# Stick-breaking mask by a restarting scan, value projections with 512 columns, and queued work shared out anew, in a two-layer hybrid decoder trunk

## The chip, the cores and the metric

The kernel runs on one core of a Trainium2 chip (trn2). The metric is the device time of one execution in microseconds. TensorE (PE in the profile) multiplies matrices and writes PSUM banks, VectorE (DVE) and ScalarE (ACT) read PSUM and SBUF, GpSimd (POOL) works on SBUF, SyncE (SP) issues the transfers from HBM.

## The reference

Two layers, each three sub-layers on a sequence of 512 tokens with 1024 features, all float32: a half-step SwiGLU, a token mixing, a half-step SwiGLU, each between two RMS norms. The mixing adds three attentions, each with a sigmoid gate: stick-breaking (8 heads of 64), forgetting (8 heads of 64) and attention to a memory of 256 tokens (4 heads of 128). Stick-breaking is the one whose mask changes:

```python
z = jnp.einsum('bhqd,bhkd->bhqk', qb, k).astype(jnp.float32) * scale
mask = key_pos[None, :] < q_pos[:, None]
log_beta = jax.nn.log_sigmoid(z)
log_not = jnp.where(mask, log_beta - z, 0.0)
log_between = lax.cumsum(log_not, axis=3, reverse=True) - log_not
w = jnp.where(mask, jnp.exp(log_beta + log_between), 0.0)
```

So a query sees the keys before it, and the weight of a key is its own sigmoid times the product of (1 - sigmoid) over the keys between. With s = softplus(z) this is exp(z - (sum of s from the key up to the last visible one)).

## The kernel before

**Numbers.** Every float32 operand of a product is split into a high and a low part in the PE's f32r format (`split`, L179: a cast on ScalarE, a difference on VectorE), and a product is three matmuls, high x high, high x low, low x high (`mm3`, L206). A weight *unit* (`Unit`, L235) is 1024 elements a partition (512 KB): it is fetched into one of two `raw` buffers by SyncE and split into one of four `wh` and four `wl` buffers. SBUF tiles of one tag share a ring of buffers (`BUFS`, L102), PSUM has two rings of four banks: `mm` for projections and outputs, `z` for scores and transposes.

**The queue.** TensorE's order is written out by a planner. `Queue` (L363) holds jobs, each a list of weight units and a generator; each step of the generator emits some matmuls and yields the time it thinks they take (columns / 2370, in us; "planned us" below). When a job begins, its units are loaded and up to four units of the next jobs are loaded ahead. Beside the queue run *chains* (L446, `weave`): a chain emits its own work on TensorE, yields `("pe", us)`, and then `("wait", us)`: for so long the planner fills in steps of the queue, up to a `limit` (an index into the queue). When the queue has come to the limit, the plan skips the rest of the wait and the chain's next piece follows at once. The waits are constants: `W_H`, `W_U` (L602) at the seams between sub-layers, `W_MM0`, `W_MM1`, `W_SB0`, `W_SB1`, `W_FL`, `W_FX0`, `W_FX1`, `W_K` (L1076 to L1080) in the mixing. `Q.past(n, us)` runs the queue to job n and `us` into it; `Q.until(n)` to job n. Instructions of the other engines are put in order by the framework's scheduler.

**The seams.** When a half of the down projection of a token tile is done (`down`, L777), a chain (L591) computes its residual and norm, waits `W_H` and `W_U[t]`, transposes the tile on TensorE (`turned`, L586) and splits the result. The next SwiGLU begins with a pair of column blocks in two halves of the tokens (`halved`, L631), the second of which needs all four tiles.

**The mixing** (`mixing`, L1108) queues per layer: memory keys and values (`mem_kv`, L872), memory queries, q, k and v of the stick-breaking and the forgetting heads, gates and branch products (`merge`), then the output projection. Heads go in pairs p = 0 to 3 with j = 0, 1. Over the queue run the chains: four memory heads (`mem_head`), eight stick heads (`stick_head`, L950), eight forgetting heads (`fox_head`, L999). Each has three pieces on TensorE: scores (`zm`, `zs`, `zf`), transposes of the weights (`ptm`, `pts`, `ptf`; `transposed`, L940), product with the values (`pvm`, `pvs`, `pvf`; `attend`, L926). The first stick head's scores are begun during the last memory head's wait (L1301).

**Values.** `vproj` (L897) puts two token tiles of 256 value columns side by side into one PSUM bank; for every tile and feature block the activations are the stationary operand and 256 weight columns stream past (L907 to L909). Memory values go through it in two groups of columns (`values`, L884). Stick and forgetting values too, in groups of two head pairs (`v_half`, from L1145, called by `project_v`, L1173): stick group 0 before head 0, stick group 1 behind head 0's other work, forgetting group (1,0) later. The first forgetting group goes with the eight forget-gate columns (`v_gates`, 264 columns).

**The mask.** `masks16` holds two bf16 triangles of 0 and -1e30 (`more_constants`, L138). A stick head writes them into three PSUM banks by four matmuls with the identity (L958), then adds the scores (L964). Per bank, ScalarE and VectorE form softplus (L969 to L972), `tensor_tensor_scan` (L976) runs from the last key backwards with state = 1 x state + s, and L978 and L979 subtract and take Exp. A masked score of -1e30 has a softplus of 0 and an Exp of 0. Forgetting heads use the other triangle in the same way (L1005).

Of the kernel before, what the change touches and what calls it, by code (L numbers as in the profile page):

```python
# [22 lines left out]
def kernel(  # L23
# [66 lines left out]
    ident16 = cst.tile([P, P], BF16, name="ident16")  # L90
# [4 lines left out]
    masks16 = cst.tile([P, P + 1], BF16, name="masks16")  # L95
    causal16, strict16 = masks16[:, 0:P], masks16[:, 1:P + 1]
# [41 lines left out]
    def more_constants():  # L138
        later = tc.keep_in_program_order
        later(nc.vector.tensor_copy(ident16[:], ident[:]))  # L140

        t0 = tmp("c0")
        later(nc.vector.memset(t0[:, :P + 1], 0.0))
        nc.gpsimd.affine_select(out=t0[:, 256:257 + P], in_=t0[:, :P + 1], pattern=[[-1, P + 1]], compare_op=ALU.is_ge,
                                fill=-1e30, base=0, channel_multiplier=1)
        later(nc.vector.tensor_copy(masks16[:], t0[:, 256:257 + P]))
# [455 lines left out]
    W_H, W_U = 4.8, (8.0, 7.0, 6.5, 6.5)  # L602
# [269 lines left out]
    def mem_kv(l, mn, ks, vs):  # L872

        mact = lambda k: (mn[0][:, k], mn[1][:, k])

        def keys(c, un):
            kt = stile([P, 2, 2, M], "v", f"mk{l}_{c}")
            for m in range(2):
                pt = pbank("mm", f"pmk{l}_{c}_{m}")
                yield from gemm(pt[:, :M], un, m, mact)  # L880
                split(kt[:, 0, m], kt[:, 1, m], pt[:, :M])
            ks.append(kt)

        def values(c, un):  # L884
            vt = stile([P, 2, MT, 256], "v", f"mv{l}_{c}")
            pt = yield from vproj(un, mact, range(MT), f"pmv{l}_{c}")
            split(vt[:, 0].rearrange("p t c -> p (t c)"), vt[:, 1].rearrange("p t c -> p (t c)"), pt[:])
            vs.append(vt)
# [4 lines left out]
        un = [wpair(w_mem_kv[l], ND, 512 + c * 256, f"mv{l}_{c}") for c in range(2)]  # L893
        Q.add(un[0], lambda: values(0, un[0]))
        return lambda: Q.add(un[1], lambda: values(1, un[1]))

    def vproj(units, act, tiles, name):  # L897

        pt = pbank("mm", name)
        for i, t in enumerate(tiles):  # L900
            o = pt[:, i * 256:(i + 1) * 256]
            ts_ = slice(t * P, (t + 1) * P)
            for un in units:
                for k in range(un.nk):
                    ah, al = act(un.k0 + k)
                    first = i == 0 and un.k0 + k == 0
                    nc.tensor.matmul(o, ah[:, ts_], un.h[:, k], start=first, stop=False)  # L907
                    nc.tensor.matmul(o, ah[:, ts_], un.l[:, k], start=False, stop=False)
                    nc.tensor.matmul(o, al[:, ts_], un.h[:, k], start=False, stop=(i == 1 and un.k0 + k == ND - 1))  # L909
                    yield 768 * PE_US  # L910
        return pt
# [14 lines left out]
    def attend(pv, j, vts, pj, tri, ot, name):  # L926

        r, rl, _ = HEAD_ROWS[j]
        for kt in range(NT):
            lo = QLO[kt]  # L930
            v = vts[kt // 2][:, 2 * (kt % 2) + pj, 2 * j:2 * j + 2, :].rearrange("p e c -> p (e c)")
            for part in range(2):
                nc.tensor.matmul(pv[:, lo:], v, tri_part(tri, part, kt, kt * P - lo), start=(kt == 0 and part == 0),
                                 stop=(kt == NT - 1 and part == 1), skip_group_check=True)
# [15 lines left out]
    def stick_head(q, k, vts, pj, j, ot, name, late):  # L950
# [5 lines left out]
        for rows, pz in zip(banks, pzs):  # L956
            for n, (i, at) in enumerate(rows):
                nc.tensor.matmul(pz[:, at + i * P:at + (i + 1) * P], ident16[:], strict16, start=n == 0, stop=False,  # L958
                                 skip_group_check=True)
        for rows, pz in zip(banks, pzs):  # L960
            for i, at in rows:
                wp = max((i + 1) * P, 256)
                for kk in (j, 2 + j):
                    nc.tensor.matmul(pz[:, at:at + wp], q[:, j, i * P:(i + 1) * P], k[:, kk, :wp], start=False,  # L964
                                     stop=(kk == 2 + j), skip_group_check=True)
# [19 lines left out]
        attend(pbank("mm", "pv" + name), j, vts, pj, wt, ot, name)  # L985
# [13 lines left out]
    def fox_head(q, k, vts, pj, j, qk, ot, name, ahead):  # L999

        rc = slice(0, 104 if j == 0 else P)
        ptile = {}
        pzs = [pbank("z", f"z{name}_{i}") for i in range(NT)]
        for i, pz in enumerate(pzs):
            nc.tensor.matmul(pz[:, i * P:(i + 1) * P], ident16[:], causal16, start=True, stop=False,  # L1005
                             skip_group_check=True)
        for i in reversed(range(NT)):
# [6 lines left out]
            st = sb.tile([P, 2], F32, tag="st", bufs=8, name=f"st{name}_{i}")  # L1014
# [12 lines left out]
        attend(pbank("mm", "pv" + name), j, vts, pj, tri, ot, name)  # L1027
        yield ("pe", 1.2)

    def mem_head(q, ks, vs, hd, ot, name, begun):  # L1030
# [37 lines left out]
        for kt in range(MT):  # L1068
            c = slice(kt * S, (kt + 1) * S)
            vc = slice((hd % 2) * P, (hd % 2 + 1) * P)  # L1070
            v = vs[hd // 2]
            mm3(pv[:], v[:, 0, kt, vc], v[:, 1, kt, vc], tri[:, 0, c], tri[:, 1, c], kt == 0, kt == MT - 1)
# [3 lines left out]
    W_SB0, W_SB1 = 11.0, 4.7  # L1076
    W_FL = 3.0
    W_FX0, W_FX1 = 6.0, 4.2
    W_MM0, W_MM1 = 6.0, 6.0
# [28 lines left out]
    def mixing(l, src, ks, vs, rest, dst):  # L1108
# [36 lines left out]
        def v_half(br, c, un):  # L1145
            for i in range(NT // 2):
# [3 lines left out]
                pt = yield from vproj(un, act, (2 * i, 2 * i + 1), f"pv{l}_{br}_{c}_{i}")  # L1150
# [88 lines left out]
        marks["values"] = rest()  # L1239
# [8 lines left out]
        marks[heads[0]] = len(Q.jobs)  # L1248
        for i, (br, _) in enumerate(heads):
# [6 lines left out]
            if i % 2 == 0 and i + 2 < len(heads):  # L1256
# [17 lines left out]
        def run():  # L1274
# [5 lines left out]
            def mems():  # L1280
# [13 lines left out]
                for i in range(NMH):  # L1294
# [24 lines left out]
            def fox(at, j):  # L1319
                pre(at, j)  # L1320
                p = FOX[at]
                return fox_head(st["q", 1, p], st["k", 1, p], st["v", 1, p // 2], p % 2, j, fx[p, j], st["o", 1][p],
# [117 lines left out]
    for l in LAYERS:  # L1440
# [3 lines left out]
        rest = mem_kv(l, mn, *kvs[l])  # L1444
        mb = mixing(l, subs[i + 1], *kvs[l], rest, subs[i + 2])
# [38 lines left out]
```

## Time and profile before

| | |
|---|---|
| median of 3 runs | 2443.98 us (2442.83 to 2444.6) |
| the profiled execution | 2443.11 us |
| its span, first to last instruction | 2441.3 us |
| granted TensorE clock, mean | 0.999 |
| instructions | 30918, of them 12167 matmuls |
| from HBM | 272.20 MB, 114 GB/s over the span, reads and writes |

In the rows of a timeline stand the start from the span's start, the duration in us, engine, line, operation, what it writes <- reads, the shape, how many rows were merged, and in brackets the idle time before it with what ended it. Matmuls overlap in the pipeline: a printed duration is longer than the distance to the next one. In a row of groups stand, after the count, busy us, mean ns of one, and idle us of the engine before them. In a row of waits stand who waited for whom, total us, how often, and the longest. Tile names are without buffer numbers (`pv` is a bank of a value projection, `pmv` of a memory value projection).

### The profile page before, as it was taken

The numbers are of one execution on the slowest core, as the hardware profiler recorded it, in microseconds if no ns is written. First come the engines' busy times: TensorE is split into PE (matmuls) and PEld (weight loads), VectorE is DVE, ScalarE is ACT, GpSimd is POOL, SyncE is SP. The second block draws the span as 40 slices with busy tenths as digits, with TensorE's granted clock in tenths as the row PEclk, the third lists the DMA queues.
The fourth block names the chain that finished last, engine by engine and source line by source line (L and its number), as shares of the span: only waits on it lengthen the run. The fifth ranks groups of instructions, "written<-read, shape, count | busy, mean of one in ns | idle before, by whom it ended". The sixth has DMA issues, their size and how long they took to land.

```text
span 2441.3 us, 30918 instructions
## 1 busy us (share of the span) xinstructions
PE 2429.5 (100%) x12167; PEld 2062.0 (84%) x12167; DVE 1544.3 (63%) x2182; ACT 1173.4 (48%) x1897; POOL 72.6 (3%) x129
## 2 busy tenths in 40 slices
PE   9999999999999999999999999999999999999998
PEld 8888889888888888888888888899888888888887
DVE  4364777677876653646644546866778866445466
ACT  4333365567655543333433333546676655333333
POOL 0000000001110000000000000000001100000000
PEclk9999999999999999999999999999999999999999
DMA  4333445222213433333424343442232243333433
GB/s 139 116 126 130 136 158 155 74 74 70 87 61 120 139 104 112 124 127 127 158 87 130 113 144 131 166 128 70 70 96 69 71 137 129 96 130 105 145 115 128
DMA packets 238597, 280.50 MB, mean 115 GB/s; under 512 B 8666, under 2 KB 188914, under 8 KB 238452
## 3 DMA queue, kind: packets, MB, share of 16 engines
q1 hardware_dynamic: 238356, 278.50, 35.5%
q8 instruction: 95, 1.56, 0.3%
q14 instruction: 50, 0.41, 0.0%
q0 software_dynamic: 96, 0.03, 0.0%
HBM read 272.20 MB, written 6.29 MB: 114 GB/s over the span
## 4 chain that ended last, share of the span: by engine, by line
PE 94%; DVE 2%; ACT 2%; DMA 1%; issue 1%; DVEq 0%; ACTq 0%
PE pg L208 4%; PE pg L210 4%; PE pg L209 4%; PE pgc L208 3%; PE pgc L210 3%; PE pgc L209 3%; PE puc L208 3%; PE puc L209 3%; PE puc L210 3%; PE pga L208 3%; PE pga L210 3%; PE pua L210 3%; PE pga L209 3%; PE pda L209 3%; PE pua L209 3%; PE pda L208 3%
## 5 line engine op out<-in xcount | busy, mean ns | idle before, releaser
L208 PE MATMUL pg<-us_a,wh_wg 128*128 128x512 f32 x384 | 150.7, 392 | 0.0
L209 PE MATMUL pg<-us_a,wh_wg 128*128 128x512 f32 x384 | 149.8, 390 | 0.0
L210 PE MATMUL pg<-us_a,wl_wg 128*128 128x512 f32 x384 | 149.6, 390 | 0.0
L208 PE MATMUL pgc<-us_b,wh_gc 128*128 128x512 f32 x320 | 124.5, 389 | 0.0
L209 PE MATMUL pgc<-us_b,wh_gc 128*128 128x512 f32 x320 | 124.5, 389 | 0.0
L210 PE MATMUL pgc<-us_b,wl_gc 128*128 128x512 f32 x320 | 124.5, 389 | 0.0
L210 PE MATMUL puc<-us_b,wl_uc 128*128 128x512 f32 x320 | 124.5, 389 | 0.0
L208 PE MATMUL puc<-us_b,wh_uc 128*128 128x512 f32 x320 | 124.5, 389 | 0.0
L209 PE MATMUL puc<-us_b,wh_uc 128*128 128x512 f32 x320 | 124.5, 389 | 0.0
L183 DVE TENSOR_TENSOR wl_uc<-raw_uc,wh_uc 128x1024 fp32r<-128x1024 f32 x44 | 53.9, 1225 | 107.3 <-ACT wh_uc L182 107.3
L183 DVE TENSOR_TENSOR wl_ua<-raw_ua,wh_ua 128x1024 fp32r<-128x1024 f32 x44 | 53.8, 1224 | 99.1 <-ACT wh_ua L182 99.1
L182 ACT CAST wh_uc<-raw_uc 128x1024 fp32r<-128x1024 f32 x44 | 46.3, 1052 | 88.8 <-PE pgc L209 37.7
L183 DVE TENSOR_TENSOR wl_gc<-raw_gc,wh_gc 128x1024 fp32r<-128x1024 f32 x40 | 48.8, 1223 | 62.1 <-ACT wh_gc L182 61.8
L210 PE MATMUL pda<-wh_da,ala 128*128 128x512 f32 x224 | 87.1, 389 | 0.0
L209 PE MATMUL pda<-wl_da,aha 128*128 128x512 f32 x224 | 87.1, 389 | 0.0
L208 PE MATMUL pdc<-wh_dc,ahc 128*128 128x512 f32 x224 | 87.1, 389 | 0.0
L209 PE MATMUL pdc<-wl_dc,ahc 128*128 128x512 f32 x224 | 87.1, 389 | 0.0
L208 PE MATMUL pda<-wh_da,aha 128*128 128x512 f32 x224 | 87.1, 389 | 0.0
L210 PE MATMUL pdc<-wh_dc,alc 128*128 128x512 f32 x224 | 87.1, 389 | 0.0
L183 DVE TENSOR_TENSOR wl_ga<-raw_ga,wh_ga 128x1024 fp32r<-128x1024 f32 x40 | 48.7, 1222 | 59.8 <-ACT wh_ga L182 59.7
L182 ACT CAST wh_ua<-raw_ua 128x1024 fp32r<-128x1024 f32 x44 | 46.1, 1050 | 81.0 <-PE pga L209 35.8
L210 PEld LDWEIGHTS pg<-us_a,wl_wg 128*128 128x128 f32 x384 | 72.1, 188 | 15.1
(466 smaller groups left out, 7245.5 us busy)
## 6 DMA issues: line engine op xcount, KB each, us to landing
raw_da<-in_ffn_w_down_dram SPq DMA_DIRECT2D x58, 512.0 KB, 3.3
raw_dc<-in_ffn_w_down_dram SPq DMA_DIRECT2D x58, 512.0 KB, 3.2
raw_wg<-in_w_gate_dram SPq DMA_DIRECT2D x48, 512.0 KB, 3.5
raw_ga<-in_ffn_w_gate_dram SPq DMA_DIRECT2D x44, 512.0 KB, 3.6
raw_ua<-in_ffn_w_up_dram SPq DMA_DIRECT2D x44, 512.0 KB, 3.6
raw_gc<-in_ffn_w_gate_dram SPq DMA_DIRECT2D x44, 512.0 KB, 3.7
raw_uc<-in_ffn_w_up_dram SPq DMA_DIRECT2D x44, 512.0 KB, 3.6
raw_wo<-in_w_out_dram SPq DMA_DIRECT2D x24, 512.0 KB, 3.2
```

Source lines behind the costliest of these rows:

```text
L182: both = [nc.scalar.copy(h_ap, src)]
L183: make = lambda: nc.vector.tensor_tensor(l_ap, src, h_ap.bitcast(F32), ALU.subtract)
L208: nc.tensor.matmul(pt, lh, rh, start=start, stop=False, skip_group_check=free)
L209: nc.tensor.matmul(pt, lh, rl, start=False, stop=False, skip_group_check=free)
L210: nc.tensor.matmul(pt, ll, rh, start=False, stop=stop, skip_group_check=free)
```

## The change

- *Mask.* The four mask matmuls of a stick head go; its first score matmul opens the bank. The scan starts with a state of 1e30, and its first operand is a row of `begins16`: 1 everywhere, 0 at the last visible key of a query. At the zero the state restarts, so keys behind it keep about 1e30 and get an Exp of 0. `begins16` is made at the start by a memset, a select on GpSimd and a cast, over 512 columns. `ident16` is no longer a tile of its own but every second 16-bit half of `ident`.
- *Values.* `vproj` takes one token tile, a bank and up to 512 columns. Memory values are two jobs over half the features each, with two banks open across both. The stick values of all four pairs are one job (`v_all`) of four units with 512 columns, ahead of head 0; `attend` gets a function that picks a pair's columns. Forgetting values keep 256 columns (and 264).
- *Sharing out.* New constants for `W_U`, `W_SB0` and `W_MM1`; `W_FL` becomes `W_MORE`, which for three heads adds to `W_SB0`. Head (0,0)'s scores begin 6.5 planned us after its keys, inside `v_all`; `Q.until(marks["v"])` ends that job before the head's first wait.
- Besides, memory keys fill one bank for both halves and are split once, and the forgetting heads' statistics share one tile.

```diff
-    ident16 = cst.tile([P, P], BF16, name="ident16")
+    ident16 = ident[:].bitcast(BF16)[:, 1::2]
...
-    masks16 = cst.tile([P, P + 1], BF16, name="masks16")
-    causal16, strict16 = masks16[:, 0:P], masks16[:, 1:P + 1]
+    causal16 = cst.tile([P, P], BF16, name="causal16")
+
+    begins16 = cst.tile([P, S], BF16, name="begins16")
...
+        t2, t3 = tmp("c2"), tmp("c3")
+        later(nc.vector.memset(t2[:], 1.0))
+        nc.gpsimd.affine_select(out=t3[:], in_=t2[:], pattern=[[-1, S]], compare_op=ALU.not_equal,
+                                fill=0.0, base=S - P - 1, channel_multiplier=1)
+        later(nc.vector.tensor_copy(begins16[:], t3[:]))
...
-    W_H, W_U = 4.8, (8.0, 7.0, 6.5, 6.5)
+    W_H, W_U = 4.8, (8.0, 7.0, 7.0, 5.7)
...
+        def values(un):
+            if un[0].k0 == 0:
+                pvs.extend(pbank("mm", f"pmv{l}_{t}") for t in range(MT))
+            for un1 in un:
+                for t, pt in enumerate(pvs):
+                    yield from vproj(un1, mact, t, pt)
+            if un[0].k0 > 0:
+                for t, pt in enumerate(pvs):
+                    vs.append(stile([P, 2, S], "v", f"mv{l}_{t}"))
+                    split(vs[t][:, 0], vs[t][:, 1], pt[:])
...
+        un = [Unit(w_mem_kv[l], k, 2, S, S, f"mv{l}_{k}") for k in range(0, ND, 2)]
+        Q.add(un[:2], lambda: values(un[:2]))
+        return Q.add(un[2:], lambda: values(un[2:]))
...
+    def vproj(un, act, t, pt):
+
+        ts_ = slice(t * P, (t + 1) * P)
+        for k in range(un.nk):
+            kk = un.k0 + k
+            ah, al = act(kk)
+            mm3(pt[:, :un.ncol], ah[:, ts_], al[:, ts_], un.h[:, k], un.l[:, k], kk == 0, kk == ND - 1)
+            yield 3 * un.ncol * PE_US
...
-                nc.tensor.matmul(pz[:, at + i * P:at + (i + 1) * P], ident16[:], strict16, start=n == 0, stop=False,
-                                 skip_group_check=True)
-        for rows, pz in zip(banks, pzs):
-            for i, at in rows:
                 wp = max((i + 1) * P, 256)
                 for kk in (j, 2 + j):
-                    nc.tensor.matmul(pz[:, at:at + wp], q[:, j, i * P:(i + 1) * P], k[:, kk, :wp], start=False,
-                                     stop=(kk == 2 + j), skip_group_check=True)
+                    nc.tensor.matmul(pz[:, at:at + wp], q[:, j, i * P:(i + 1) * P], k[:, kk, :wp],
+                                     start=(n == 0 and kk == j), stop=(kk == 2 + j), skip_group_check=True)
...
-                nc.vector.tensor_tensor_scan(back, one_t[:].broadcast_to([P, n]), back, 0.0, ALU.mult, ALU.add)
+
+                nc.vector.tensor_tensor_scan(back, begins16[:, S - 1:S - 1 - n if n < S else None:-1], back, 1e30,
+                                             ALU.mult, ALU.add)
...
-            nc.tensor.matmul(pz[:, i * P:(i + 1) * P], ident16[:], causal16, start=True, stop=False,
+            nc.tensor.matmul(pz[:, i * P:(i + 1) * P], ident16, causal16[:], start=True, stop=False,
...
-    W_SB0, W_SB1 = 11.0, 4.7
-    W_FL = 3.0
+    W_SB0, W_SB1 = 12.0, 4.7
+
+    W_MORE = {(0, 0): -5.5, (NP - 1, 0): 2.0, (NP - 1, 1): 1.0}
     W_FX0, W_FX1 = 6.0, 4.2
-    W_MM0, W_MM1 = 6.0, 6.0
+    W_MM0, W_MM1 = 6.0, 4.5
...
+        def v_all(br, un):
+            for t in range(NT):
+
+                vt = stile([P, 4, 4, HD], "v", f"v{l}_{br}_{t}")
+                st.setdefault(("v", br), []).append(vt)
+                pt = pbank("mm", f"pv{l}_{br}_{t}")
+                for un1 in un:
+                    yield from vproj(un1, act, t, pt)
                 split(vt[:, :, 0:4:3, :], vt[:, :, 1:3, :], pt[:].rearrange("p (a e c) -> p a e c", a=4, e=2))
...
-            if (br, p) == (1, FOX[0]):
+            if br == 0:
+                un = [Unit(w_in[l], k, 2, base, S, f"v{l}_{br}_{k}") for k in range(0, ND, 2)]
+                Q.add(un, lambda: v_all(br, un))
+            elif (br, p) == (1, FOX[0]):
...
-        marks[heads[0]] = len(Q.jobs)
+        marks["v"] = len(Q.jobs)
...
-            if i % 2 == 0 and i + 2 < len(heads):
+            if i in (2, 4):
                 project_v(*heads[i + 2])
...
-                            Q.past(marks[0, 0], W_K, marks[0, 1])
+                            Q.past(marks[0, 0], W_K + 2.5, marks[0, 1])
...
-                return stick_head(st["q", 0, p], st["k", 0, p], st["v", 0, p // 2], p % 2, j, st["o", 0][p], f"s{l}_{p}_{j}",
-                                  W_FL if (p, j) == (NP - 1, 0) else 0.0)
+                return stick_head(st["q", 0, p], st["k", 0, p], lambda kt: st["v", 0][kt][:, p], j, st["o", 0][p], f"s{l}_{p}_{j}",
+                                  W_MORE.get((p, j), 0.0))
...
+                if p == 0:
+                    Q.until(marks["v"])
```

More of the change, by code (lines that the diff above doesn't have):

```diff
@@ L877, in keys @@
             kt = stile([P, 2, 2, M], "v", f"mk{l}_{c}")
+            pt = pbank("mm", f"pmk{l}_{c}")
             for m in range(2):
-                pt = pbank("mm", f"pmk{l}_{c}_{m}")
-                yield from gemm(pt[:, :M], un, m, mact)
-                split(kt[:, 0, m], kt[:, 1, m], pt[:, :M])
-            ks.append(kt)
[L884 to L888, printed above, removed]
+                for un1 in un:
+                    for k in range(un1.nk):
+                        kk, cols = un1.k0 + k, slice(m * P, (m + 1) * P)
+                        ah, al = mact(kk)
+                        mm3(pt[:, m * M:(m + 1) * M], un1.h[:, k, cols], un1.l[:, k, cols], ah, al, m == 0 and kk == 0,
+                            m == 1 and kk == ND - 1, free=True)
+                        yield 3 * M * PE_US
+            split(kt[:, 0], kt[:, 1], pt[:].rearrange("p (e m) -> p e m", e=2))
+            ks.append(kt)
+        pvs = []
+        def values(un):
[8 more added lines that the diff above has]
+                    split(vs[t][:, 0], vs[t][:, 1], pt[:])
         for c in range(2):
@@ L924, in tri_part, with attend @@
         return t[:, n:n + NT - kt]
-    def attend(pv, j, vts, pj, tri, ot, name):
+    def attend(pv, j, value, tri, ot, name):
         r, rl, _ = HEAD_ROWS[j]
@@ L1237, in merge @@
             return Q.add(ub, run)
-        marks["values"] = rest()
+        marks["values"] = values
         for c in range(2):
```

64 lines of the change are left out of this document (28 added, 36 removed).

## The prediction

> **What bounds the kernel now.** I read the first parts of the page, then the chain that ended last, then TensorE's timeline in the stages that the diff touches.
>
> ```profile
> span 2441.3 us, 30918 instructions
> ...
> PE 2429.5 (100%) x12167; PEld 2062.0 (84%) x12167; DVE 1544.3 (63%) x2182; ACT 1173.4 (48%) x1897; POOL 72.6 (3%) x129
> ```
> ```profile
> PE 94%; DVE 2%; ACT 2%; DMA 1%; issue 1%; DVEq 0%; ACTq 0%
> ```
>
> TensorE is busy for all but 11.8 us and carries 94% of the last chain; VectorE has a third of the span free, ScalarE half. So two things count: how long the stream of matmuls is, and where it stops. A busy TensorE is not a full one, so I take the distance from start to start, not the printed duration.
>
> ```profile
> 446.10 0.28 PE L909 MATMUL pv<-wh_v,us_a 128*128 128x256 f32 x1
> ...
> 451.86 0.28 PE L909 MATMUL pv<-wh_v,us_a 128*128 128x256 f32 x1
> ...
> 453.36 0.39 PE L208 MATMUL pq<-us_a,wh_q 128*128 128x512 f32 x1
> ...
> 456.08 0.39 PE L208 MATMUL pq<-us_a,wh_q 128*128 128x512 f32 x1
> ```
>
> Between the first two rows lie 48 steps of 256 columns: 5.76/48 = 0.120 us each. Between the last two lie 12 steps of 512 columns: 2.72/12 = 0.227. Two matmuls of 256 columns cost 0.240, one of 512 costs 0.227: **0.013 us saved a pair** for the same columns.
>
> **Value projections.** Which pairs join:
>
> ```profile
> L907 PE MATMUL pv<-wh_v,us_a 128*128 128x256 f32 x192 | 54.6, 285 | 0.0
> ```
> ```profile
> L907 PE MATMUL pmv<-wh_mv,mn 128*128 128x256 f32 x64 | 18.4, 288 | 0.0
> ```
>
> Each step issues three matmuls (L907 to L909): 576 and 192. Of the 576, two of the three groups a layer that go through `v_half` are stick-breaking: 384. Memory's 192 all join. That makes 192 + 96 = 288 pairs, 288 x 0.013 = 3.7 us. The fox groups keep their shape. Bytes, splits and weight units stay as many: a unit is 1024 elements a partition, before as 4 x 256, after as 2 x 512.
>
> A page of the Trainium skill speaks against this term: "TensorE: Matmul & The Clock Gate", section "Wait — 56ns, not 53.3ns?", puts the start-to-start distance at columns / 2.4 GHz plus about 2.5 ns. By it a pair would save some 2.5 ns, the 288 pairs an estimated 0.7 us. The trace disagrees: 0.227 and 0.120 leave about 13 ns beyond the columns for these matmuls, and the trace decides.
>
> **The mask.** A head's four mask matmuls and its scores:
>
> ```profile
> L958 PE MATMUL zs<-masks,ident 128*128 128x128 bf16 x64 | 6.4, 223 | 0.0
> ```
> ```profile
> 484.94 0.40 PE L958 MATMUL zs<-masks,ident 128*128 128x128 bf16 x4
> 485.15 1.54 PE L964 MATMUL zs<-k,q 128*128 128x512 f32 x8
> 486.53 0.28 PE L907 MATMUL pv<-wh_v,us_a 128*128 128x256 f32 x1
> ```
>
> The block takes 486.53 - 484.94 = 1.59 us. The eight score matmuls alone (two each of 512 and 384 columns, four of 256) take 2 x 0.227 + 2 x 0.174 + 4 x 0.120 = 1.28, with 0.174 halfway between the two measured steps. So 0.31 a head, for 16 heads 4.9 us. Counted only from the first mask to the first score it would be 0.21 a head, 3.4 us. I take 4.9, as the whole block has to fit between its neighbours.
>
> The scan keeps its instructions and elements and gets another first operand. The new constant costs VectorE and GpSimd at the start:
>
> ```profile
> 28.35 0.30 POOL L144 TENSOR_SCALAR_AFFINE_SELECT c<-c 128x129 f32<-128x129 f32 x1 [21.62 <-DVE c L143]
> ```
> ```profile
> 29.77 2.36 DVE L183 TENSOR_TENSOR wl_ga<-raw_ga,wh_ga 128x1024 fp32r<-128x1024 f32 x2
> 35.66 1.22 DVE L183 TENSOR_TENSOR wl_ua<-raw_ua,wh_ua 128x1024 fp32r<-128x1024 f32 x1 [3.54 <-ACT wh_ua L182]
> ```
>
> A select of 512 columns takes 0.3 to 1.2 us; VectorE's copy waits for it, and behind the copy stand the low halves at 29.77. With memset and copy that is about 2 us, less than the 3.54 that VectorE then idles: nothing; without that cover 2 us. `ident16` becomes a strided view, loaded for the 64 fox masks (L1005). No row shows a strided load: between nothing and another 0.05 each, 3.4 us. I take nothing, since loads lie beside matmuls here (PEld overlaps PE).
>
> **Shared-out work: the stops that go.**
>
> ```profile
> 540.84 0.39 PE L210 MATMUL pk<-us_a,wl_k 128*128 128x512 f32 x1
> 541.31 1.31 PE L946 MATMUL pts<-ident,ts 128*128 128x128 f32 x10
> ```
> ```profile
> 628.47 1.31 PE L946 MATMUL pts<-ident,ts 128*128 128x128 f32 x10 [1.13 <-ACT ts L979]
> ```
> ```profile
> L946 PE MATMUL pts<-ident,ts 128*128 128x128 f32 x160 | 20.3, 274 | 1.4 <-ACT ts L979 1.1
> ```
>
> A stick head's transposes come before its last Exp (L979). At 541.31, head (1,1), they start 0.47 after the last matmul where 0.23 is usual: 0.24 lost. At 628.47, head (3,1), 1.13 of idle stands, 1.28 in start-to-start. The 0.3 that the group's idle has left is three times the 0.08 of the first, so I count three stops of 0.24 in all: 2.0 us. After, these heads wait 12 and 13 planned us instead of 11, so the transposes come 1 to 2 us later and all 2.0 go.
>
> ```profile
> 879.41 1.04 PE L586 MATMUL utb<-ident,fb 128*128 128x128 f32 x8
> 880.20 0.36 PE L648 MATMUL puc<-us_b,wh_uc 128*128 128x256 f32 x1
> ```
> ```profile
> 884.12 1.04 PE L586 MATMUL utb<-ident,fb 128*128 128x128 f32 x8
> 885.40 0.38 PE L651 MATMUL pgc<-us_b,w_gc 128*128 128x256 f32 x1 [0.25 <-ACT us_b L185]
> ```
> ```profile
> 1233.80 1.07 PE L586 MATMUL utc<-ident,fc 128*128 128x128 f32 x8 [0.22 <-DVE fc L576]
> ...
> 1239.34 0.39 PE L651 MATMUL pga<-us_c,w_ga 128*128 128x256 f32 x1 [0.25 <-ACT us_c L185]
> ```
>
> At the seams between sub-layers the last tile's transposes end just when the first half's work is used up: 1.28 us to the next start against 0.79 for the tile before, 0.49 lost, at 885, 1239 and layer 1's twin of 885. With W_U[3] 0.8 smaller the transposes come while some 0.65 planned us of that work is left, which covers the split: 3 x 0.49 = 1.5. W_U[2] 0.5 larger covers the stop at 1233.80, 0.37 in start-to-start. Together 1.9 us.
>
> **Shared-out work: the stop that comes.** All stick values now stand ahead of head 0, so 10.4 planned us (32 steps of 0.324) leave head 0's stage as filler, and five heads take 1 us more each. Head (3,0) may use filler up to `before (1,3)`. Now:
>
> ```profile
> 608.25 1.26 PE L946 MATMUL pts<-ident,ts 128*128 128x128 f32 x10
> 609.26 0.48 PE L208 MATMUL pg<-us_a,wh_wg 128*128 128x512 f32 x1
> ```
> ```profile
> 612.76 1.44 PE L933 MATMUL pvs<-pts,v 128*128 128x512 f32 x8
> ```
> ```profile
> 609.23 1.03 ACT L182 CAST wh_k<-raw_k 128x1024 fp32r<-128x1024 f32 x1
> 610.29 1.42 ACT L182 CAST pts<-pts 128x512 fp32r<-128x512 f32 x4
> ```
> ```profile
> 610.29 1.23 DVE L183 TENSOR_TENSOR wl_k<-raw_k,wh_k 128x1024 fp32r<-128x1024 f32 x1 [0.25 <-ACT wh_k L182]
> 611.44 1.68 DVE L183 TENSOR_TENSOR pts<-pts,pts 128x512 fp32r<-128x512 f32 x4
> ```
>
> From 609.26 to 612.76 are 3.5 us of filler between transposes and `attend`. After, the work ahead of that limit is 7 x 0.31 + 96 x 0.013 = 3.4 us shorter, while the transposes come only 0.6 to 1.6 earlier (head 0's first wait ends 5 earlier, five heads take 5.2 more, six masks take 1.8 off, and each wait is rounded up to a whole step). So 0.7 to 1.7 us of filler are left, and `attend` waits for the splits. Above: the first part is ready as late as here (about 612.1, 3.9 after the transposes began, against 1.0 + 0.7), 2.2 lost. Below: without the casts ahead of it (1.03 and 1.23) it is ready some 2 us sooner, 0.3 lost. Those casts wait for buffers that the filler frees, and the filler ends earlier now, so I take the middle, 1.2 a layer: **2.4 us lost**.
>
> The value job also holds all four weight buffers (`wh`, `wl`). The next unit can be split when its last tile has passed unit 0, 18 matmuls or 4.1 us before its end; the split needs 1.03 + 1.23. The fourth unit likewise has 4.1 us from the end of k00. But a cast that waits for a buffer holds up ScalarE:
>
> ```profile
> ACT wh_wg L185 <- PE pv L909: 12.0, 10, 3.5
> ```
>
> The longest such wait is 3.5 us, and Exps stand behind it. Between nothing and 3.5 a layer; I take 0.5 in all, near nothing, as TensorE did not stop for any of these ten. Head (0,0)'s transposes have over 20 us after its scores (the rest of the value job, 15, and 6.5).
>
> **Sum.** -3.7 - 4.9 - 2.0 - 1.9 + 2.4 + 0.5 = -9.6 us. The profiled execution took 2443.11 us (span 2441.3, 1.8 around it); the median of three runs is 2443.98, 0.9 higher. That gives 2433.5 by the one and 2434.4 by the other: **2434 us**.
>
> **Rivals.**
>
> 1. *The gain is given back at the new waits* (chance 0.14): 2.2 a layer at head (3,0) and 3.5 a layer behind casts, the stops at (1,1) and (3,1) unchanged. At the worst -3.7 - 4.9 - 1.9 + 4.4 + 7.0 = +0.9, so 2439 to 2445 us. For it: filler already falls short there (3.5 us for a wait of 4.7). Against: few such places.
> 2. *Slower: the value job starves what is behind it* (0.06). One mechanism: four units in four buffers. If ScalarE has the casts of q01, k01 and the gates ahead of memory's and the head's work, TensorE stops at the fourth unit (2.3 for its split), at the last memory head (3.5) and at q01 (2.3): 8.1 a layer, 16.2 in all, less the 0.5 above: -9.6 + 15.7 = +6.1, 2450 us. Slower than before from 5.1 a layer. Against: the q and k units change one in 5.4 us (24 x 0.227) today without a stop.
> 3. *Joining saves nothing* (0.05): the value matmuls keep 0.240 for 512 columns, because of their loads. 2434 + 3.7 = 2437.7 us. Against: q's matmuls load new weights each too, at 0.227. The Trainium skill's rule above comes near this case, with 2437.
>
> **How the numbers follow.** Forecast 0.75, rivals 0.14, 0.06, 0.05. Without the new waits -12.5, 2431.5 us; one us more for small starts behind the bf16 blocks gives 2430 as the lower end. Upwards the waits' upper ends (+2.0 and +6.5) give 2442.5, and the start and the strided loads lie within that: 2430 to 2442 leaves out the slower rival and the rim of the first. About 0.2% (4.9 us) is what a measurement of this kernel can tell from no change. Faster by more: 0.75 + 0.05 = 0.80; within: 0.14; slower: 0.06.
>
> **What would show it.** 352 matmuls fewer; no mask group in the stick heads; value matmuls of 512 columns at 0.227; score blocks of 1.28; no stop before `pts` of heads (1,1) and (3,1) nor at the three seams; a new stop of about 1.2 us before `pvs` of head (3,0) in each layer. Wrong would be a stop inside or right after the value job, scans that last longer, or fox masks that move apart.

## The result and the profile after

| | before | after |
|---|---|---|
| median of 11 runs each, side by side | 2443.98 us | 2437.76 us (2435.9 to 2440.4) |
| the profiled execution | 2443.11 us | 2440.4 us |
| its span | 2441.3 us | 2438.7 us |
| matmuls | 12167 | 11815 |

The ratio is 0.9975, with an interval of 0.9967 to 0.9983: faster by 6.2 us, where 9.6 were forecast. The profiled execution of the changed kernel is the longest of its eleven, so its trace shows less of the gain than a usual run; a second one (`after_again`, span 2435.4) stands with the experiments. A head (p, j) below is the stick head j of pair p; a stop is idle time of TensorE in its stream.

The first part of the page and the shares of the last chain:

```profile
span 2438.7 us, 30173 instructions
...
PE 2423.5 (99%) x11815; PEld 2043.7 (84%) x11815; DVE 1546.6 (63%) x2179; ACT 1173.1 (48%) x1893; POOL 74.4 (3%) x130
```
```profile
PE 96%; DVE 1%; ACT 1%; DMA 1%; issue 0%; DVEq 0%; SPq 0%; ACTq 0%
```

TensorE bounds as before, with 352 matmuls fewer (96 + 192 joined, 64 masks). Its timeline in the value job of layer 0, and then around head (0,1)'s scores:

```profile
454.70 0.39 PE L214 MATMUL pv<-wh_v,us_a 128*128 128x512 f32 x1
...
459.92 0.39 PE L216 MATMUL pv<-wh_v,us_a 128*128 128x512 f32 x1
```
```profile
479.55 1.46 PE L972 MATMUL zs<-k,q 128*128 128x512 f32 x8
480.85 0.40 PE L214 MATMUL pg<-us_a,wh_wg 128*128 128x512 f32 x1
```

23 steps in 5.22 us are 0.227 each. The score block takes 480.85 - 479.55 = 1.30, before 1.59. The scan's group of 512 columns, before and after:

```profile
L976 DVE TENSOR_TENSOR_SCAN ts<-one_t,ts 128x512 f32<-128x512 f32 x16 | 19.5, 1218 | 0.3
```
```profile
L985 DVE TENSOR_TENSOR_SCAN ts<-begins,ts 128x512 f32<-128x512 bf16 x16 | 19.6, 1224 | 0.5
```

The restarting scan costs next to nothing (1224 against 1218 ns). At the first seam of layer 0 the stop of 0.49 is gone: the next start follows the last tile's transposes by 0.79.

```profile
881.19 1.03 PE L592 MATMUL utb<-ident,fb 128*128 128x128 f32 x8
881.98 0.36 PE L654 MATMUL puc<-us_b,wh_uc 128*128 128x256 f32 x1
```

What is new stands in TensorE's waits, none of which the kernel before had, and in the six places of its timeline where they lie:

```profile
PE pvs L945 <- ACT pts L188: 3.1, 3, 1.5
PE pvs L945 <- DVE pts L189: 2.1, 3, 0.8
```
```profile
591.41 0.39 PE L945 MATMUL pvs<-pts,v 128*128 128x256 f32 x1 [0.81 <-DVE pts L189]
...
610.84 0.51 PE L945 MATMUL pvs<-pts,v 128*128 128x512 f32 x1 [0.99 <-ACT pts L188]
...
613.72 0.38 PE L945 MATMUL pvs<-pts,v 128*128 128x256 f32 x1 [0.62 <-ACT pts L188]
...
1799.38 0.50 PE L945 MATMUL pvs<-pts,v 128*128 128x256 f32 x2 [0.47 <-DVE pts L189]
...
1800.70 0.39 PE L945 MATMUL pvs<-pts,v 128*128 128x256 f32 x1 [0.81 <-DVE pts L189]
...
1824.41 0.39 PE L945 MATMUL pvs<-pts,v 128*128 128x256 f32 x1 [1.52 <-ACT pts L188]
```

All are products with the values that wait for the split of the transposes. 610.84, 613.72 and 1824.41 belong to head (3,0), where one stop was forecast. 591.41, 1799.38 and 1800.70 belong to head (2,1), where none was. From start to start they lose 6.3 us in all. Behind the pair at 1800 TensorE also runs slower for a while, as the windows of 4 us show (the column after the engines' busy times is the granted clock):

```profile
1797.00:1801.00 4.00, 2.72 (x12) 1.66 (x12) 3.56 (x6) 2.14 (x6) 0.00 (x0) 1.00 0.47 131
1801.00:1805.00 4.00, 4.00 (x15) 3.46 (x14) 3.56 (x5) 3.68 (x7) 3.57 (x5) 0.57 0.10 13
```

That costs another 1.6: the score block there takes 2.18 instead of 1.30, and three steps of 512 columns 0.43 instead of 0.227.

Why head (2,1)? ScalarE and VectorE in layer 0, from the transposes (at 582.65) to the stop:

```profile
586.28 0.68 ACT L1105 ACTIVATE fa<-pfl,bfor 8x512 f32<-8x512 f32 x1
586.86 0.56 ACT L188 CAST pts<-pts 128x512 fp32r<-128x512 f32 x1
587.33 0.63 ACT L1106 ACTIVATE fa<-fa 8x512 f32<-8x512 f32 x1
587.86 0.45 ACT L188 CAST pts<-pts 128x384 fp32r<-128x384 f32 x1
588.22 0.72 ACT L1107 ACTIVATE fa<-fa,one_t 8x512 f32<-8x512 f32 x1
588.84 0.51 ACT L188 CAST pts<-pts 128x256 fp32r<-128x256 f32 x2
```
```profile
588.97 0.74 DVE L1108 SCALAR_TENSOR_TENSOR fa<-pfl,nbfor,fa 8x512 f32<-8x512 f32 x1
589.64 0.40 DVE L189 TENSOR_TENSOR pts<-pts,pts 128x256 fp32r<-128x256 f32 x1
589.97 1.20 DVE L1109 TENSOR_TENSOR_SCAN fb<-bfor,fa 8x512 f32<-8x512 f32 x1
591.10 0.25 DVE L189 TENSOR_TENSOR pts<-pts,pts 128x128 fp32r<-128x128 f32 x1
```

Between the four splits stand the steps of the forget gate's cumulative sum (`fa`, `fb`): its job in the queue now comes just ahead of these transposes. The last difference starts at 591.10, behind the scan, and TensorE goes on at 591.41.

### The profile page after: what moved, and what is told of

The parts are those of the page before. It is cut to its first block, busy times and chain, and to the rows that moved or that the text cites. A ratio compares the mean times of both kernels' runs of the same rounds, so it can differ in the third digit from the quotient of the medians.

```text
span 2438.7 us, 30173 instructions
## 1 busy us (share of the span) xinstructions
PE 2423.5 (99%) x11815; PEld 2043.7 (84%) x11815; DVE 1546.6 (63%) x2179; ACT 1173.1 (48%) x1893; POOL 74.4 (3%) x130
## 3 DMA queue, kind: packets, MB, share of 16 engines
q8 instruction: 93, 1.52, 0.3%
## 4 chain that ended last, share of the span: by engine, by line
PE 96%; DVE 1%; ACT 1%; DMA 1%; issue 0%; DVEq 0%; SPq 0%; ACTq 0%
PE pg L215 3%; PE pg L214 3%; PE pg L216 3%; PE pga L214 3%; PE pgc L214 3%; PE puc L214 3%; PE pga L215 3%; PE pga L216 3%; PE pda L214 3%; PE pua L216 3%; PE pua L215 3%; PE pda L215 3%; PE puc L216 3%; PE pda L216 3%; PE pgc L216 3%; PE pgc L215 3%
## 5 line engine op out<-in xcount | busy, mean ns | idle before, releaser
L189 DVE TENSOR_TENSOR wl_ua<-raw_ua,wh_ua 128x1024 fp32r<-128x1024 f32 x44 | 53.8, 1224 | 98.4 <-ACT wh_ua L188 98.4
```

Of the source, the lines that this page charges most:

```text
L189: make = lambda: nc.vector.tensor_tensor(l_ap, src, h_ap.bitcast(F32), ALU.subtract)
```

## The experiments

**Theory A**: the savings came as forecast, and what is missing was lost at (2,1) and (3,0), for want of filler and by the place of the cumulative sum. **B**: the savings themselves are smaller. The ratio of every run is to the kernel before, timed beside it on the same chip. The chips differ: the median of the kernel before was 2443.98 us beside the changed kernel, 2442.91 in experiments 1, 2, 5 and 6, 2445.00 in 3, 4, 8 and 9, 2442.85 in 7 and 10, and 2441.87 in 11 and 12. So the distance to the changed kernel is given between the medians and, behind it in brackets, between the two gains over the kernel before. Where the two differ, the distance is known no better than that.

**1. More filler left for the later heads (`filler_back`).**

```diff
-    W_MORE = {(0, 0): -5.5, (NP - 1, 0): 2.0, (NP - 1, 1): 1.0}
+    W_MORE = {(0, 0): -10.0, (NP - 1, 0): 2.0, (NP - 1, 1): 1.0}
```

> The changed kernel, with the head (0,0) waiting for 2.0 planned us of filler instead of 6.5, so that 4.5 planned us more are left for the heads behind it. The changed kernel's trace shows stops before the `pvs` of head (2,1) (0.97 us in layer 0; 0.73 and 0.97 in layer 1) and of head (3,0) (1.16 and 0.79; 1.69), some 7 us in all, and a granted clock of 0.57 for 4 us behind the stop in layer 1. Theory A (the savings in the stream came as forecast, and the difference to the forecast is these stops, for want of filler): the stops at (3,0) go, 3.6 us, those at (2,1) stay unless their splits come earlier; 2434 us or less, 2432 if (2,1) goes as well. Rival B (the stream saved less than forecast, the stops are covered by something else that is late): within 1 us of the changed kernel, 2437. Rival C (head (0,0)'s last Exps now come too late for its transposes, since the filler stood there for a reason): a new stop before `pts` of head (0,0), and slower than the changed kernel, 2439 or more.

2432.68 us, ratio 0.9956 (0.9942 to 0.9970): 5.1 (4.0) less than the changed kernel, theory A. All stops before `pvs` are gone, and the granted clock stays at 1.00 in the mixing. Besides two of 0.2 at head (1,1), one stop before transposes is left, at head (3,0) of layer 1:

```profile
1809.78 0.33 PE L958 MATMUL pts<-ident,ts 128*128 128x128 f32 x1 [1.23 <-ACT ts L989]
```

At (3,0) filler is what was added: from transposes to product it is 6.5 us in layer 0 (603.48 to 610.02), where the changed kernel has 2.95 with its stop. At (2,1) it is not: 6.37 (579.54 to 585.91) against 6.58. There the heads now come earlier against the queue, and the cumulative sum lies behind the splits of (2,1), as in the kernel before (sum from 590.26, casts of the splits until 587.64):

```profile
580.23 1.42 ACT L188 CAST pts<-pts 128x512 fp32r<-128x512 f32 x4 [1.96 <-PE pts L958]
...
585.50 0.66 ACT L1105 ACTIVATE fa<-pfl,bfor 8x512 f32<-8x512 f32 x1
```

**2. The cumulative sum one job later (`cumsum_later`).**

```diff
-                if (br, p, x) == (1, FOX[0], "q"):
+                if (br, p, x) == (1, FOX[0], "k"):
```

> The changed kernel, with the job of the forget gate's cumulative sum queued behind the k projection of the first fox pair, one unit (5.4 us) later than now. Theory A (at head (2,1) the sum's Exp, Ln and scan stand between the transposes' splits on ScalarE and VectorE, and `pvs` waits for them): the stops before `pvs` of (2,1) go (0.97 in layer 0, 0.73 and 0.97 in layer 1) and with them the lower granted clock behind them (1.5 us); the stops at (3,0) stay as they are or grow: 2434 to 2436 us. Rival B (the splits are late by themselves, the sum only stands beside them): the stops stay, within 1 us of 2437.8. Rival C (the sum now meets head (3,0), or the fox attention waits for it): 2439 or more.

2434.87 us, 0.9968 (0.9955 to 0.9980): 2.9 (1.8) less, theory A. Nothing stops at (2,1); at (3,0) two shorter stops stay:

```profile
610.14 0.50 PE L945 MATMUL pvs<-pts,v 128*128 128x512 f32 x1 [0.69 <-DVE pts L189]
...
611.60 0.39 PE L945 MATMUL pvs<-pts,v 128*128 128x256 f32 x1 [0.20 <-DVE pts L189]
```

**3. Both edits (`both`).**

> The changed kernel with both edits of the first series: head (0,0) waits for 2.0 planned us instead of 6.5, and the cumulative sum is queued behind the k projection. Alone they gave 2432.7 and 2434.9 against 2437.8. Theory A (one want of filler, which either edit eases at head (2,1), and only the first at (3,0)): nothing is left for the second edit at (2,1) or at `pvs` of (3,0); what it can still take away is the stop of 1.2 us that the first edit's trace has before `pts` of head (3,0) in layer 1, if the sum's instructions are what makes those Exps late: 2431.5 to 2432.7. Rival B (the two edits have different causes): the gains add up, -5.1 - 2.9 = -8.0, 2430. Rival C (the sum, later, now meets the Exps or splits of head (3,0)): 2434 or more.

2433.53 us, 0.9953 (0.9939 to 0.9967): 4.2 (5.3) less than the changed kernel. The times can't tell A from B: between the medians the second edit adds nothing, between the gains the two nearly add up (4.0 + 1.8 = 5.8). The traces say more: at (2,1) both edits do the same thing, they bring the sum behind the splits, and there nothing was left to gain. The stop of 1.23 before `pts` went, and one of 0.34 came at `pg`, which waits for the sum on VectorE.

**4. The first edit turned round (`filler_less`).**

```diff
+    W_MORE = {(0, 0): -1.5, (NP - 1, 0): 2.0, (NP - 1, 1): 1.0}
```

> The changed kernel with head (0,0) waiting for 10.5 planned us instead of 6.5, so that 4.0 planned us less filler are left for the heads behind it: the first series' edit turned round. Theory A (the stops before `pvs` are want of filler): the filler before `attend` of (3,0) is gone, so its first part stands open by the whole 3.8 us of its split less what lies in between, at least 0.8 more than now a layer, and the head behind it, or (2,1), loses what is left of the 4.0: 1.6 to 8 us slower than the changed kernel, 2439.4 to 2446. Rival B (the stops come from the casts' order on ScalarE and VectorE alone): within 1 us of 2437.8.

2446.09 us, 1.0008 (0.9999 to 1.0016): 8.3 (7.3) slower than the changed kernel, at the upper end of A. With the first edit this is a curve: 4.0 planned us less filler cost 7 to 8 us, 4.5 more gain 4 to 5. TensorE's waits:

```profile
PE pvs L945 <- ACT pts L188: 6.1, 2, 3.1
PE pfl L1101 <- DVE fl L1153: 2.5, 2, 1.4
```

Each layer has one stop of 3 us before `attend` of (3,0), and behind it the lower clock, as these starts of 512-column matmuls show (0.42 apart):

```profile
613.98 0.79 PE L945 MATMUL pvs<-pts,v 128*128 128x512 f32 x1 [2.98 <-ACT pts L188]
...
615.00 0.63 PE L215 MATMUL pq<-us_a,wh_q 128*128 128x512 f32 x1
615.42 0.63 PE L216 MATMUL pq<-us_a,wl_q 128*128 128x512 f32 x1
```

From start to start the stops of the mixing lose 11.1 us in this trace and the lower clock 4.5, against 6.3 and 1.6 in the first trace of the changed kernel.

**5. The mask alone, on the kernel before (`mask_alone`).** All of the mask's diff, and the shared statistics tile for room; nothing of values, waits or order. Its core:

```diff
-                nc.tensor.matmul(pz[:, at + i * P:at + (i + 1) * P], ident16[:], strict16, start=n == 0, stop=False,
-                                 skip_group_check=True)
...
-                nc.vector.tensor_tensor_scan(back, one_t[:].broadcast_to([P, n]), back, 0.0, ALU.mult, ALU.add)
+                nc.vector.tensor_tensor_scan(back, begins16[:, S - 1:S - 1 - n if n < S else None:-1], back, 1e30,
+                                             ALU.mult, ALU.add)
```

> The kernel before, with the mask by the restarting scan alone: no mask matmuls in the stick-breaking heads, the scan's first operand the new constant, the fox masks through the strided identity. Values stay at 256 columns, the queue and its waits as before. Theory A (each head's score block is 0.29 to 0.31 shorter, the scan and the strided load cost nothing): -4.6 to -4.9 us, 2439.2, less what the stops before `pts` of (1,1) and (3,1) grow by when the scores come earlier (up to 0.3 a head and layer, 1.2). Rival B (the mask saves only the time from the first mask to the first score, 0.21 a head): -3.4 us, 2440.6. Rival C (scan or fox masks cost it back): within 1 us of 2444.

2441.34 us, 0.9992 (0.9983 to 1.0001): -1.6, less gain than A or B had. The stream is 0.29 shorter a head, 16 x 0.29 = 4.6 us, but heads whose scores come earlier reach their transposes before their Exps:

```profile
PE pts L952 <- ACT ts L982: 3.7, 6, 1.0
```

From start to start these six stops lose 4.7, where the kernel before lost 2.0; the two at head (1,0), 0.9 each, are new. The growth of 2.7 is more than the 1.2 I had allowed: -4.6 + 2.7 = -1.9. Without longer waits, over half of the mask's gain is lost.

**6. The value matmuls halved again (`values_256`).** In the changed kernel:

```diff
-            mm3(pt[:, :un.ncol], ah[:, ts_], al[:, ts_], un.h[:, k], un.l[:, k], kk == 0, kk == ND - 1)
+            for c in HALVES:
+                mm3(pt[:, c], ah[:, ts_], al[:, ts_], un.h[:, k, c], un.l[:, k, c], kk == 0 and c.start == 0,
+                    kk == ND - 1 and c.start > 0, free=True)
```

> The changed kernel, with each value matmul of 512 columns issued as two of 256; the order, the units, the queue and its planned times unchanged. This takes the joining back alone. Theory A (a pair costs 0.240, the joint matmul 0.227): 288 pairs x 0.013 = 3.7 us slower than the changed kernel, 2441.5. Rival B (joining saves the 2.5 ns a matmul that the Trainium skill's page names): the next sentence has its number. By the page "TensorE: Matmul & The Clock Gate" it would be an estimated 0.7 us, 2438.5. Rival C (TensorE has cover for the longer stream, since the stops at heads (2,1) and (3,0) shrink when the filler gets longer): less than 3.7, down to nothing.

2439.68 us, 0.9985 (0.9976 to 0.9994): 1.9 (3.0) slower than the changed kernel, which doesn't tell A from C. But C's reason isn't there: the stops at (2,1) and (3,0) lose 4.8 us here and 4.8 in `after_again`. The same points of the same work in `after_again` and in this kernel (start of the memory sub-layer's transposes, first memory scores, head (0,1)'s scores):

```profile
368.66 0.38 PE L592 MATMUL uta<-ident,fa 128*128 128x128 f32 x2
...
404.76 0.28 PE L214 MATMUL zm<-mk,qm 128*128 128x256 f32 x1
...
479.78 0.40 PE L972 MATMUL zs<-k,q 128*128 128x512 f32 x1
```
```profile
368.18 0.38 PE L592 MATMUL uta<-ident,fa 128*128 128x128 f32 x2
...
404.85 0.28 PE L214 MATMUL zm<-mk,qm 128*128 128x256 f32 x1
...
481.18 0.40 PE L974 MATMUL zs<-k,q 128*128 128x512 f32 x1
```

The stage with the memory values takes 36.67 instead of 36.10 (+0.57; the kernel before has 36.68), the one with the stick values 76.33 instead of 75.02 (+1.31). In layer 1 it is +0.53 and +1.31: 3.7 us in the program. Joining gives what was forecast; to the end, these two executions also differ in the start (0.9 us less here) and in the stop at `mt` (0.5 more), which the edit doesn't touch. The Trainium skill ("TensorE: Matmul & The Clock Gate", section "Wait — 56ns, not 53.3ns?") has 2.5 ns beyond the columns, which made an estimated 0.7 us; the trace disagrees, with 3.7.

**7. The same on the kernel of experiment 1 (`filler_back_256`).**

> The kernel of `filler_back` with each value matmul of 512 columns issued as two of 256. On the changed kernel the same edit cost 1.9 us in the medians and 2.6 between two profiled executions, where the stages with the value matmuls grew by 0.6 and 1.3 a layer, 3.7 in all. Theory A (the whole 3.7 is in the stream, and what was missing at the end were the stops and seams around it, which take up part of any shift): between 2.6 and 3.7 slower than `filler_back`, 2435.3 to 2436.4. Rival B (joining is worth only the 1.9 to the end): 2434.6 or less.

2435.58 us, 0.9971 (0.9960 to 0.9983): 2.9 (3.0) slower than `filler_back`, theory A. The two stages of layer 0 take 36.66 instead of 36.11 and 71.57 instead of 70.26, as in experiment 6.

**8. The seams alone, on the kernel before (`seams_alone`).**

```diff
-    W_H, W_U = 4.8, (8.0, 7.0, 6.5, 6.5)
+    W_H, W_U = 4.8, (8.0, 7.0, 7.0, 5.7)
```

> The kernel before, with the waits W_U at the seams as in the change (7.0 and 5.7 for the last two tiles) and nothing else. Theory A (the stops of 0.49 at the three seams and the stop of 0.37 before tile 2 go, as in the changed kernel's trace, where 0.26 of the latter is left): -1.5 to -1.9 us against the kernel before, 2441.2. Rival B (the last tile's transposes come earlier but then wait for their own normed rows, or the first tile of the next stage is late): within 0.5 us of the kernel before.

2442.61 us against 2445.00 of the kernel before, 0.9991 (0.9983 to 1.0000). That is -2.4, with an interval down to nothing. In the trace the three stops of 0.49 are gone, as theory A has it. But a stop came that neither the kernel before nor the changed one has, at the second tile of the middle seam, which waits for its normed rows as in rival B:

```profile
1220.60 1.09 PE L586 MATMUL utc<-ident,fc 128*128 128x128 f32 x8 [1.35 <-DVE fc L576]
```

The span of this execution is 2440.7, only 0.6 under that of the kernel before. So that the stops go is shown; what they are worth to the end is not.

**9. The changed kernel once more (`after_again`).**

> The changed kernel again, for a second profiled execution. In the first, which took 2440.4 us, the granted clock was 0.57 for 4 us behind two stops of 0.73 and 0.97 us at head (2,1) of layer 1, and 1.00 behind a single stop of 0.97 at the same head in layer 0. Theory A (the clock falls when enough idle lies close together): the stops of layer 1 are again two, and the clock falls again; or there is one, and it stays. Rival B (the clock falls by chance): a fall in another place or behind a single stop, or none behind two.

2437.12 us. Each layer now has one stop at (2,1), and the clock stays at 1.00 in the mixing. That fits theory A; experiment 10 has a fall behind a single stop.

```profile
591.01 0.39 PE L945 MATMUL pvs<-pts,v 128*128 128x256 f32 x1 [0.24 <-DVE pts L189]
...
1798.37 0.39 PE L945 MATMUL pvs<-pts,v 128*128 128x256 f32 x1 [0.20 <-DVE pts L189]
...
1817.80 0.50 PE L945 MATMUL pvs<-pts,v 128*128 128x512 f32 x1 [0.98 <-ACT pts L188]
```

So the stops at (3,0) belong to the kernel (1.9 and 2.1 us a layer from start to start), while those at (2,1) vary (0.4 here, 1.0 and 1.7 before).

**10. Still more filler (`filler_more`).**

```diff
+    W_MORE = {(0, 0): -12.0, (NP - 1, 0): 3.5, (NP - 1, 1): 1.0}
```

> The kernel of `filler_back` with 2.0 planned us more filler moved: head (0,0) waits for nothing (its transposes had 8.7 us to spare in that trace), head (3,0) for 15.5 instead of 14. `filler_back` took 2432.7 and its trace has one large stop left, 1.39 us from start to start before `pts` of (3,0) in layer 1. Theory A (filler is what was short): that stop goes, `pvs` of (3,0) keeps its cover, 2431.3 us. Rival B (those Exps are late because of what the filler itself puts on VectorE and ScalarE, so more filler makes them later still): within 0.7 of 2432.7. Rival C (head (0,0) now starts its transposes before something else that it needs): 2434 or more.

2437.57 us, 0.9980 (0.9971 to 0.9989): 4.9 slower than `filler_back`, by none of the three reasons.

```profile
572.21 0.76 PE L958 MATMUL pts<-ident,ts 128*128 128x128 f32 x5 [1.96 <-ACT ts L989]
572.73 0.37 PE L214 MATMUL pv<-wh_v,us_a 128*128 128x264 f32 x1
```

These are half of the transposes of (2,1). The other half follows 39 matmuls of the forgetting values later (at 577.55), while in `filler_back` all ten stand together behind these values. So the built order has half of them further forward, where their Exps aren't done; I take it that the framework's scheduler drew them there. TensorE waits 1.96 for them, in both layers, and in layer 1 the clock falls for 3.41 us behind it, which costs another 1.6.

**11. Small corrections (`filler_even`).**

```diff
+    W_MORE = {(0, 0): -10.0, (1, 1): 0.3, (NP - 1, 0): 3.0, (NP - 1, 1): 1.0}
```

> The kernel of `filler_back` with small corrections at the stops that its trace has left: head (1,1) waits 12.3 instead of 12 planned us (stops of 0.20 before its `pts`, twice), head (3,0) 15 instead of 14 (1.39 in layer 1); head (0,0) stays at 2. In the built order every head's transposes stand together, unlike in `filler_more`. Theory A (what `filler_more` lost, it lost by transposes drawn ahead of their Exps, and a little more wait where a stop is left pays): 0.4 us for (1,1), up to 1.4 for (3,0): 2431 to 2432.3. Rival B (the stop at (3,0) is not in every execution, and no filler is left for it): 2432.3 to 2433.5. Rival C (the filler for the last heads runs out again): 2434 or more.

2432.50 us, 0.9960 (0.9946 to 0.9973): the same as `filler_back`, rival B. The stop at (3,0) of layer 1 is gone, but the wait of (1,1) was not lengthened by a step, and its two stops of 0.20 stay.

**12. `filler_back` once more (`filler_back_again`).**

> The kernel of `filler_back` again, for a second profiled execution. The first has a stop of 1.39 us before `pts` of head (3,0) in layer 1 and none at that head in layer 0, though both layers run the same program. Theory A (these Exps end within some tenths of the transposes in every execution, and what SyncE's loads and the casts behind them do decides it): the stop comes in one layer, in both or in none, and its size is another. Rival B (layer 1 has something that layer 0 lacks): the same stop in the same place.

2433.43 us; the same stop in the same place, a little shorter, which is nearer to rival B:

```profile
1809.00 0.33 PE L958 MATMUL pts<-ident,ts 128*128 128x128 f32 x1 [0.98 <-ACT ts L989]
```

In layer 1 these Exps end 17.4 us after the head's scores, in layer 0 16.0. What delays them was not tried.

## Why the prediction was near, and where it failed

The time lies inside the range; the gain is two thirds of the forecast. That is partly luck: the loss at (2,1) has no term of its own in the sum, and the range covers it only because it allowed up to 6.5 us for casts behind the value job, where nothing was lost. Point by point, sizes from start to start:

| term | forecast | measured | by |
|---|---|---|---|
| values | -3.7 | -3.7 | the stages in experiment 6 |
| mask | -4.9 | -4.6 | score blocks, experiment 5 |
| stops at (1,1) and (3,1) | -2.0 | -2.0 | the trace after |
| seams | -1.9 | -1.6 | the trace; 0.26 is left before tile 2 of one seam |
| new stops | +2.4 and +0.5 | +4.8, +7.9 | `after_again`; the first trace (6.3, and 1.6 by the clock) |

The first four sum to -11.9 and stand. The sum with `after_again` is -7.1; its span is 5.9 under that of the kernel before. In that execution the start took 0.6 more (the first matmuls, `gqx`, wait 1.0 for a DMA), and a stop of 0.6 that the kernel before has at `mt`, and that lies between 0 and 1.1 in the executions here, is missing. So 1.2 us are not assigned. The new `W_MM1`, the 2.5 added to `W_K` and the single bank of the memory keys, for which the sum has no terms, were not tried alone.

What failed is the step "the stop that comes". At (3,0) its working was right (0.78 us of filler between transposes and `attend`, where 0.7 to 1.7 were worked out), and the choice within its bounds wrong: 1.9 to 2.1 us a layer, near the upper 2.2, not the middle. I had taken the middle between a split as late as before and an undisturbed one, but a gate's steps and a cast that waits for its DMA stand between the parts. And the step looked at one head only. Work that leaves the queue's front moves every later job against the heads, and the cumulative sum came to lie among the splits of (2,1); experiment 2 shows that this alone is worth some 1.8 to 2.9, and in experiment 1 the loss at (2,1) goes for the same reason, not by more filler. The slower clock was not foreseen.

Rival 1 named this mechanism, but put over half of its price behind casts that wait for buffers, where nothing stopped. Rivals 2 and 3 are dead: no stop lies in or right behind the value job, and joining saves its 13 ns. Whether the start costs anything is not shown: up to the first `mt` the two traces of the changed kernel took 0.4 and 0.6 more than the kernel before, but those of `both` and `mask_alone`, which make the same constant, 0.7 and 1.1 less. The strided load cost nothing (96 to 101 ns a load, before 95 to 101).

Experiment 1 closes the account: with the new stops taken away by one constant it gains 10.2 us over the kernel before beside it, and -11.9 with its remaining stops of 1.4 and twice 0.2 makes -10.1 (its profiled execution, the longest of five, is 8.7 shorter). At the other end, -11.9 with the 15.6 us that `filler_less` loses makes +3.7, and its span is 3.9 over that of the kernel before. Experiment 1 is also, with experiments 3 and 11, the best version found.

## What to carry to other kernels

A change that shortens TensorE's stream under a written-out order pays only where the chains beside it have time to spare. Measure that first, for every head: from the last Exp to the transposes, from the last split to the product. When work is taken from the front of a queue, go through all jobs behind it and see between whose steps they now fall. Medians of different chips differed here by up to 3 us for the same kernel, as much as the terms; compare the stages of two traces, not only the ends.

## What the runs showed of the hardware

At some stops of TensorE in the mixing the granted clock fell to 0.50 for 3.41 us, once for 6.83. While it was down, matmuls of 512 columns started every 0.427 us instead of 0.227. It fell behind two stops of 0.47 and 0.81 us (the first trace, at 1801.10), within a single one of 2.98 (`filler_less`, at 613.02), behind one of 3.15 (the same, at 1828.16) and behind one of 1.96 (`filler_more`, at 1779.84), but not at single ones of 1.52 (the first trace) and 1.43 (`filler_less`).

The length of a stop alone doesn't decide, for `filler_more` stops for 1.96 us at the same place of both layers, and the clock fell in layer 1 only. The changes of the clock lie on a fixed grid: in these three traces it rises at 1804.52, 619.85 and 1783.25 and next falls 631.47, 1208.32 and 648.53 us later, which are 185, 354 and 190 steps of 3.4133 us. These are the stretches of that grid around the two stops, layer 1 first (the second number is TensorE's busy time, the one behind the engines the clock):

```profile
1776.43:1779.84 3.41, 1.45 (x13) 1.24 (x13) 3.41 (x10) 2.31 (x5) 0.00 (x0) 1.00 0.26 90
1779.84:1783.25 3.41, 3.41 (x18) 3.41 (x17) 1.33 (x3) 0.71 (x2) 0.00 (x0) 0.50 0.00 0
```
```profile
568.11:571.52 3.41, 2.14 (x18) 1.93 (x16) 3.41 (x8) 1.30 (x4) 0.00 (x0) 1.00 0.49 159
571.52:574.93 3.41, 2.72 (x23) 2.72 (x24) 2.77 (x7) 2.00 (x5) 0.00 (x0) 1.00 0.00 0
```

In layer 1 the whole stop lies in one stretch, and the clock falls at its end; in layer 0 an edge of the grid cuts it into 1.27 and 0.69. So it counts how much of a stop falls into one stretch, and the same program can meet the grid differently. Idle time isn't all of it: a stretch with 1.28 us idle was followed by a fall (the two stops of the first trace), stretches with 1.43 and 1.52 were not, and why stays open.

The Trainium skill ("TensorE: Matmul & The Clock Gate", section "What's actually happening") has the clock halve after an idle window of about 3.4 us. Its cold step of 426.7 ns for 512 columns (section "Wait — 56ns, not 53.3ns?") agrees with the trace, and so does the length of the window. But all these stops are shorter than a window: here less than a wholly idle one sufficed.
